# Turning the gated products of a feed-forward layer with VectorE and DMAs instead of TensorE

## The chip, the cores and the metric

One core of one Trainium2 chip runs the whole kernel. The metric is the device time of one execution in microseconds (us), taken as the median of the runs shown. TensorE multiplies matrices and writes to PSUM; VectorE (DVE in the profile) and ScalarE (ACT) move and combine tiles; SyncE (SP) issues the DMAs; GpSimd (POOL) has little to do here.

## The reference, cut to what matters

Two layers run over 256 tokens of width 2048. Each has a mixer (attention and a gated recurrence), a feed-forward part, and a gated embedding part. The change lies in the feed-forward part, whose inner width `D_FF` is 5632:

```python
h = rms_norm(x, pre_ffn_gain[i])
f = (jax.nn.silu(h @ w_ffn_gate[i]) * (h @ w_ffn_up[i])) @ w_ffn_down[i]
x = x + rms_norm(f, post_ffn_gain[i])
```

The product in the brackets (the gated product) comes out with tokens on the partitions. The multiplication by `w_ffn_down` sums over the 5632 columns, so it needs these columns on the partitions: the gated product has to be turned.

## The kernel before, in words

The 256 tokens are two tiles of 128, called t = 0 and t = 1. Every large product is made in strips of 512 output columns by `strip`. One strip walks down the rows of the weight matrix in steps of 256 rows; gate and up strips have 8 steps. For each step `load_w` loads 256x512 weights (512 KB) by one DMA on SP's queue into `wr` (4 buffers), and `split` makes of it two rounded float32r parts, `wh` by ScalarE and `wl` by VectorE (8 buffers each), which together keep the precision. TensorE then runs 12 matmuls per step, 6 for each t: left high by right high, left low by right high, left high by right low, for two blocks of 128 rows. The left operand is a turned, split tile `ck` (one high, one low).

The feed-forward part takes the 11 strips of the inner width in groups, `FF_GROUPS = (2, 3, 3, 3)`. For each strip of a group it runs a gate strip, whose end (`done_gate`, ScalarE) leaves silu of the gate in a `nat` tile, and an up strip, whose end (`done_up`) multiplies the two on VectorE. After the last strip of a group come four down strips (s = 0 to 3), which use the group's strips in order, two steps for each: a group of three has 6 steps in each down strip, and the third strip of the group is first used in step 5.

The gated product is turned by `split_T`: four TensorE transposes of 128x128 into a PSUM bank, then ScalarE copies the bank to the high part and VectorE subtracts to get the low part. `later(2, ...)` writes this code two steps after the end of the strip. Slots of a tag are given out and taken back by the framework: `nat` has 6, `ck` has 14.

The order on each engine is set when the program is built, by a list scheduler that follows the order of the code and its own estimates. On the chip, each engine works off its list in order and waits at semaphores; SP's list holds the weight loads, so a DMA that waits on SP holds back the loads behind it.

Of the kernel before, what the change touches and what calls it, by code (L numbers as in the profile page):

```python
# [8 lines left out]
F32 = mybir.dt.float32  # L9
# [6 lines left out]
P = 128  # L16
# [30 lines left out]
def decoder(ctx: ExitStack, tc: tile.TileContext, x, p, positions, w_in, attn_sinks,  # L47
# [3 lines left out]
    nc = tc.nc  # L51
# [5 lines left out]
    sp = ctx.enter_context(tc.tile_pool(name="sp", bufs=1))  # L57
    np_ = ctx.enter_context(tc.tile_pool(name="np", bufs=6))
    sm = ctx.enter_context(tc.tile_pool(name="sm", bufs=2))
    pacc = ctx.enter_context(tc.tile_pool(name="pacc", bufs=4, space=PSUM))  # L60
    pms = ctx.enter_context(tc.tile_pool(name="pms", bufs=4, space=PSUM))

    V, S, G, T = nc.vector, nc.scalar, nc.gpsimd, nc.tensor
# [7 lines left out]
    def later(n, fn):  # L71

        queue.append((clock[0] + n, fn))
# [28 lines left out]
    def nat(shape=(P, W), dt=F32):  # L102
        return np_.tile(list(shape), dt, tag="nat", name="nat")

    def bank(shape=(P, W)):
        return pms.tile(list(shape), F32, tag="ms", name="ms")
# [17 lines left out]
    ps = bank()  # L124
# [20 lines left out]
    def gain_cols(base, l, n):  # L145
        return gT[:, base + l * n: base + (l + 1) * n]
# [20 lines left out]
    def square_sum(src, acc, shape=(P, W)):  # L167
        j = np_.tile([P, W], F32, tag="junk", name="junk", bufs=1)
        S.activation(j[:, 0:shape[1]], src, AF.Square, accum_out=acc)  # L169

    def split(src, hi, lo):

        a = S.copy(hi, src)  # L173
        v = V.tensor_tensor(lo, src, hi.bitcast(F32), op=ALU.subtract)  # L174
        return a, v

    def split_wide(ps, gcols, h, lo):

        g = nat((P, 4, P))
        V.tensor_tensor(g, ps, gcols.unsqueeze(2).to_broadcast([P, 4, P]), op=ALU.mult)  # L180
        marks["x"], _ = split(g, h, lo)

    def split_T(src_blocks, gcols, hl, t, kt0=0, wide=False):

        n = len(src_blocks)
        ps = bank((P, n, P))
        for b, blk in enumerate(src_blocks):
            T.transpose(ps[:, b], blk, ident)  # L188
        h = hl[0][:, kt0:kt0 + n, t * P:(t + 1) * P]
        lo = hl[1][:, kt0:kt0 + n, t * P:(t + 1) * P]  # L190
        if gcols is None:
            split(ps, h, lo)
            return
        if wide:
            split_wide(ps, gcols, h, lo)
            return
        for b in range(n):
            g = gcols[:, b:b + 1]
            marks["x"] = S.activation(h[:, b], ps[:, b], AF.Copy, scale=g)  # L199
            V.scalar_tensor_tensor(lo[:, b], ps[:, b], g, h[:, b].bitcast(F32),  # L200
                                   op0=ALU.mult, op1=ALU.subtract)

    def new_ck():
        return [xp.tile([P, 4, SEQ], F32R, tag="ck", name="ck", bufs=14) for i in range(2)]

    def blocks4(a):
        return [a[:, b * P:(b + 1) * P] for b in range(4)]
# [11 lines left out]
    def strip(lhs, w, col, done, nch=8, row0=0, skew=0, psum=None, pre=None):  # L219

        ps = psum or [pacc.tile([P, W], F32, tag="acc", name=f"acc{t}") for t in range(NT)]
        ws = {}

        def part(t, c, lows=(0, 1)):
            hi, lo = ws[c]
            for k in range(2):
                kt = 2 * c + k
                xh, xl = (a[:, kt % 4, t * P:(t + 1) * P] for a in lhs[kt // 4])
                first, last = kt == 0, kt == 2 * nch - 1
                if 0 in lows:  # L230
                    T.matmul(ps[t], xh, hi[:, k], start=first, stop=False)  # L231
                    T.matmul(ps[t], xl, hi[:, k], start=False, stop=False)  # L232
                if 1 in lows:
                    marks[t, c] = T.matmul(ps[t], xh, lo[:, k], start=False, stop=last)  # L234

        for i in range(nch + skew):
            if pre:
                pre(i)
            if i < nch:
                with behind("x") if pre and i == 0 else nullcontext():  # L240
                    ws[i] = load_w(w, row0 // (2 * P) + i, col)
                if pre and i == 0:
                    for t in range(NT):
                        part(t, i, (0,))
                    for t in range(NT):
                        part(t, i, (1,))
                    tick()
                    continue
                part(0, i)
                if i == nch - 1:  # L250
                    done(0, ps[0])
            if i >= skew:
                part(1, i - skew)
            tick()
        done(1, ps[1])

    def load_gain(g, col):
        b = np_.tile([P, W], F32, tag="gB", name="gB", bufs=2)
        nc.sync.dma_start(b, g[col:col + W].partition_broadcast(P))
        return b  # L260

    def post_norm(mg, ss, t, nss, xT, gcols, wait):

        r = sum_rstd(ss[t], D, f"po{t}")
        for c in range(4):
            V.scalar_tensor_tensor(xr[t][c], mg[c][:, t], r[:, 0:1], xr[t][c],  # L266
                                   op0=ALU.mult, op1=ALU.add)

        def turn(cs):
            for c in cs:  # L270
                next_in(t, c, xT, gcols)
            for c in cs:
                square_sum(xr[t][c], nss[t][:, c:c + 1])
        later(wait, lambda: turn((0, 1)))
        later(wait + 1, lambda: turn((2, 3)))

    def next_in(t, c, xT, gcols, wide=False):
        split_T(blocks4(xr[t][c]), gcols[:, 4 * c:4 * c + 4], xT[c], t, wide=wide)
# [146 lines left out]
    for l in range(DEPTH):  # L425
# [385 lines left out]
        for s in range(4):  # L811
            gB = load_gain(post_mix_gain[l], s * W)

            def done(t, ps, s=s, gB=gB):
                if t == 0:
                    mg.append(sp.tile([P, NT, W], F32, tag="ABCD"[s], name=f"mg{s}"))
                V.tensor_tensor(mg[s][:, t], ps, gB, op=ALU.mult)
                square_sum(ps, ssm[t][:, s:s + 1])
                if s == 3:
                    post_norm(mg, ssm, t, ss, xT, gain_cols(32, l, 16), 4)  # L820
# [8 lines left out]
        for gi, glen in enumerate(FF_GROUPS):  # L829
            hid = []  # L830
            for j in range(glen):
                col = (ff0 + j) * W
                gate = {}

                def done_gate(t, ps):
                    gate[t] = nat()
                    S.activation(gate[t], ps, AF.Silu, scale=rx2(t)[:, 0:1])  # L837

                hl = new_ck()
                hid.append(hl)  # L840

                def done_up(t, ps):
                    V.scalar_tensor_tensor(gate[t], ps, rx2(t)[:, 0:1], gate[t],  # L843
                                           op0=ALU.mult, op1=ALU.mult)
                    later(2, lambda g=gate[t], hl=hl: split_T(blocks4(g), None, hl, t))

                strip(xT, w_ffn_gate[l], col, done_gate, skew=SKEW if ff0 + j == 0 else 0)
                strip(xT, w_ffn_up[l], col, done_up)
            last = gi == len(FF_GROUPS) - 1
            if last:  # L850
                nxT = [new_ck() for c in range(4)]
            for s in range(4):
                if gi == 0:
                    macc[s] = sp.tile([P, NT, W], F32, tag="ABCD"[s], name=f"macc{s}")
                if last:
                    gB = load_gain(post_ffn_gain[l], s * W)

                def done(t, ps, s=s):
                    m = macc[s][:, t]
                    if gi == 0:  # L860
                        S.copy(m, ps)
                        return
                    V.tensor_tensor(m, ps, m, op=ALU.add)  # L863
                    if last:
                        square_sum(m, ssf[t][:, s:s + 1])
                        V.tensor_tensor(m, m, gB, op=ALU.mult)
                        if s == 3:
                            post_norm(macc, ssf, t, nss, nxT, gain_cols(64, l, 16), (4, 3)[t])
                strip(hid, w_ffn_down[l], s * W, done, nch=2 * glen, row0=ff0 * W,
                      skew=4 if last and s == 3 else 0)  # L870
            ff0 += glen
# [67 lines left out]
```

## Time and profile before

| | us |
|---|---|
| median of 3 runs (2485.83 to 2488.48) | 2486.67 |
| the profiled execution, its own time | 2485.5 |
| span of its trace, first to last instruction | 2483.7 |
| TensorE busy in the span | 2464.8 (99%) |
| VectorE busy | 1445.0 (58%) |
| ScalarE busy | 1185.1 (48%) |

The profile's page lists busy time by engine, the chain of work that ended last, and groups of instructions. "L188" is line 188 of the kernel. A group's row shows its count, its busy time and the mean of one instruction in ns, then the idle time in front of it. Because matmuls overlap in the array, the distance from one start to the next is the price of a matmul, not its own duration. DMAs are shown by issue, with the median time from issue to landing.

### The profile page before, as it was taken

What the parts mean: (1) busy time and instruction counts of PE and PEld (TensorE: products, weight loads), DVE (VectorE), ACT (ScalarE), POOL (GpSimd) and SP (SyncE); (2) the same over time, 40 slices, a digit from 0 to 9 for tenths busy, and PEclk for the clock granted to TensorE, in tenths of its full rate; (3) what the DMA queues carried; (4) which work ended last, traced back from release to release, by engine and by line L of the source; (5) the groups of instructions that cost most, each with busy time, mean ns of one, the idle gap of its engine ahead of it and who ended that gap; (6) DMA issues with size and microseconds to landing.
All of it is one profiled execution on the core that took longest, in us unless ns stands there. A gap on an engine that the chain in (4) does not pass through costs nothing.

```text
span 2483.7 us, 30796 instructions
## 1 busy us (share of the span) xinstructions
PE 2464.8 (99%) x11597; PEld 2039.7 (82%) x11597; DVE 1445.0 (58%) x1901; ACT 1185.1 (48%) x1684; POOL 98.5 (4%) x213
## 2 busy tenths in 40 slices
PE   8999999999999999999999999999999999999999
PEld 6888887888888888887888888878888888888877
DVE  7786756544554454457567857565445545554574
ACT  6654446444434434446556444464444344444462
POOL 3100001000000000001010000010000000000010
PEclk9999999999999999999999999999999999999999
DMA  7445465666666666664564454656666666666653
GB/s 260 141 144 162 144 197 165 211 190 189 193 189 192 189 193 193 188 201 158 187 203 139 136 172 146 200 176 198 191 191 187 195 189 192 188 193 192 202 171 127
DMA packets 234262, 451.43 MB, mean 182 GB/s; under 512 B 14177, under 2 KB 15105, under 8 KB 234113
## 3 DMA queue, kind: packets, MB, share of 16 engines
q1 hardware_dynamic: 233808, 449.37, 59.1%
q8 instruction: 91, 1.49, 0.2%
q14 instruction: 59, 0.48, 0.1%
q10 hardware_dynamic: 240, 0.07, 0.0%
q0 software_dynamic: 64, 0.02, 0.0%
HBM read 447.31 MB, written 2.10 MB: 181 GB/s over the span
## 4 chain that ended last, share of the span: by engine, by line
PE 95%; DMA 2%; DVE 1%; ACT 1%; issue 0%; POOL 0%; SPq 0%; ACTq 0%; DVEq 0%; POOLq 0%
PE acc L231 29%; PE acc L232 29%; PE acc L234 29%; PE ms L188 2%; DMA wr<-in_w_in_dram 1%; PE ms L676 1%; PE ms L566 1%; DVE wl L174 1%; PE ms L515 0%; ACT wh L173 0%; PE ms L713 0%; ACT junk L169 0%; PE ms L741 0%; PE ms L232 0%; PE ms L234 0%
## 5 line engine op out<-in xcount | busy, mean ns | idle before, releaser
L174 DVE TENSOR_TENSOR wl<-wr,wh 128x1024 fp32r<-128x1024 f32 x840 | 1028.9, 1226 | 942.0 <-ACT wh L173 927.8
L173 ACT CAST wh<-wr 128x1024 fp32r<-128x1024 f32 x840 | 883.7, 1053 | 1121.2 <-PE acc L232 1068.6
L231 PE MATMUL acc<-wh,ck 128*128 128x512 f32 x3328 | 1309.8, 394 | 7.8 <-ACT ck L199 4.7
L232 PE MATMUL acc<-wh,ck 128*128 128x512 f32 x3328 | 1298.4, 390 | 0.9 <-DVE ck L200 0.8
L234 PE MATMUL acc<-wl,ck 128*128 128x512 f32 x3328 | 1297.3, 390 | 0.0
L231 PEld LDWEIGHTS acc<-wh,ck 128*128 128x128 f32 x3328 | 624.9, 188 | 139.5 <-ACT ck L199 10.1
L232 PEld LDWEIGHTS acc<-wh,ck 128*128 128x128 f32 x3328 | 625.6, 188 | 130.3 <-DVE ck L200 4.5
L234 PEld LDWEIGHTS acc<-wl,ck 128*128 128x128 f32 x3328 | 625.1, 188 | 130.8
L199 ACT ACTIVATE ck<-ms,gT 128x128 fp32r<-128x128 f32 x248 | 79.2, 368 | 35.2 <-DVE ck L200 27.7
L200 DVE SCALAR_TENSOR_TENSOR ck<-ms,gT,ck 128x128 fp32r<-128x128 f32 x248 | 75.8, 346 | 19.4 <-ACT ck L199 18.9
L159 POOL TENSOR_TENSOR tiny<-ssf 128x1 f32<-128x1 f32 x4 | 2.1, 535 | 1378.6 <-ACT junk L169 1378.3
L837 ACT ACTIVATE nat<-acc,ry 128x512 f32<-128x512 f32 x44 | 30.2, 687 | 10.7 <-PE acc L234 10.6
L863 DVE TENSOR_TENSOR macc<-acc,macc 128x512 f32<-128x512 f32 x48 | 33.0, 687 | 0.7
L169 ACT ACTIVATE junk<-x 128x512 f32<-128x512 f32 x48 | 30.2, 630 | 6.7 <-DVE x L266 4.1
L843 DVE SCALAR_TENSOR_TENSOR nat<-acc,ry,nat 128x512 f32<-128x512 f32 x44 | 32.4, 748 | 0.1
L174 DVE TENSOR_TENSOR ck<-ms,ck 128x512 fp32r<-128x512 f32 x44 | 30.1, 684 | 0.0
L188 PE MATMUL ms<-ident,x 128*128 128x128 f32 x192 | 27.8, 281 | 1.9 <-DVE x L896 1.2
L188 PEld LDWEIGHTS ms<-ident,x 128*128 128x128 f32 x192 | 22.6, 143 | 8.2 <-DVE x L896 2.4
L188 PEld LDWEIGHTS ms<-ident,nat 128*128 128x128 f32 x184 | 22.8, 139 | 6.4 <-DVE ck L200 0.4
L188 PE MATMUL ms<-ident,nat 128*128 128x128 f32 x184 | 28.0, 272 | 0.0
L459 POOL TENSOR_TENSOR nat<-nat 128x256 f32<-128x256 f32 (+1 forms) x24 | 22.7, 968 | 109.0 <-DVE nat L452 97.6
L534 ACT ACTIVATE nat<-nat,tiny 128x128 f32<-128x128 f32 x64 | 24.8, 390 | 3.9 <-DVE tiny L531 3.6
(198 smaller groups left out, 884.1 us busy)
## 6 DMA issues: line engine op xcount, KB each, us to landing
wr<-in_w_in_dram SPq DMA_DIRECT2D x176, 512.0 KB, 3.8
wr<-in_w_ffn_gate_dram SPq DMA_DIRECT2D x176, 512.0 KB, 3.8
wr<-in_w_ffn_up_dram SPq DMA_DIRECT2D x176, 512.0 KB, 3.7
wr<-in_w_ffn_down_dram SPq DMA_DIRECT2D x176, 512.0 KB, 3.7
wr<-in_w_out_dram SPq DMA_DIRECT2D x64, 512.0 KB, 4.1
wr<-in_w_ple_gate_dram SPq DMA_DIRECT2D x64, 512.0 KB, 4.3
wr<-in_w_ple_proj_dram SPq DMA_DIRECT2D x8, 512.0 KB, 4.2
x<-in_x_dram SPq DMA_DIRECT2D x8, 256.0 KB, 7.6
```

The costliest lines, as they stand in the source:

```text
L169: S.activation(j[:, 0:shape[1]], src, AF.Square, accum_out=acc)
L173: a = S.copy(hi, src)
L174: v = V.tensor_tensor(lo, src, hi.bitcast(F32), op=ALU.subtract)
L188: T.transpose(ps[:, b], blk, ident)
L199: marks["x"] = S.activation(h[:, b], ps[:, b], AF.Copy, scale=g)
L200: V.scalar_tensor_tensor(lo[:, b], ps[:, b], g, h[:, b].bitcast(F32), op0=ALU.mult, op1=ALU.subtract)
L231: T.matmul(ps[t], xh, hi[:, k], start=first, stop=False)
L232: T.matmul(ps[t], xl, hi[:, k], start=False, stop=False)
L234: marks[t, c] = T.matmul(ps[t], xh, lo[:, k], start=False, stop=last)
L837: S.activation(gate[t], ps, AF.Silu, scale=rx2(t)[:, 0:1])
L843: V.scalar_tensor_tensor(gate[t], ps, rx2(t)[:, 0:1], gate[t], op0=ALU.mult, op1=ALU.mult)
L863: V.tensor_tensor(m, ps, m, op=ALU.add)
```

## The change

The gated product is turned in two stages. VectorE turns each 32x32 block in place (`V.transpose`). The 4x4 arrangement of the blocks is then turned by DMAs: one stores the 256 KB tile to a scratch tile `turn` in DRAM, and four load it back, 64 KB each, into 32 partitions each, in runs of 128 floats (512 bytes). All five are issued on SP's queue; the four loads wait for the store to land. ScalarE and VectorE then split the loaded tile as before, now from SBUF. It is done for every strip of every group but the second strip of the group of two: 10 strips of 11, 2 tiles each, 2 layers, which is 40 turns; 4 stay on TensorE. The splitting code is written three steps after the end of a strip, not two.

```diff
+    dp = ctx.enter_context(tc.tile_pool(name="dp", bufs=4, space=bass.MemoryType.DRAM))
...
+    def shuffled(src):
+        b = nat()
+        V.transpose(b.rearrange("p (q k j) -> p k q j", q=4, k=4),
+                    src.rearrange("p (k q j) -> p k q j", k=4, q=4))
+        m = dp.tile([4, 32, 4, P], F32, tag="turn", name="turn")
+        nc.sync.dma_start(m.rearrange("a i q f -> (a i) (q f)"), b)
+        d = nat()
+        for q in range(4):
+            nc.sync.dma_start(d[q * 32:(q + 1) * 32].rearrange("i (a f) -> i a f", a=4),
+                              m[:, :, q].rearrange("a i f -> i a f"))
+        return d
+
+    def split_shuffled(d, hl, t):
+        cols = slice(t * P, (t + 1) * P)
+        split(d.rearrange("p (a k j) -> p k a j", a=4, k=4),
+              *(a[:, :, cols].rearrange("p k (a j) -> p k a j", a=4) for a in hl))
...
-                def done_up(t, ps):
+                def done_up(t, ps, hl=hl, gate=gate, j=j):
                     V.scalar_tensor_tensor(gate[t], ps, rx2(t)[:, 0:1], gate[t],
                                            op0=ALU.mult, op1=ALU.mult)
-                    later(2, lambda g=gate[t], hl=hl: split_T(blocks4(g), None, hl, t))
+                    if glen == 2 and j == 1:
+                        later(2, lambda g=gate[t], hl=hl: split_T(blocks4(g), None, hl, t))
+                        return
+                    d = shuffled(gate[t])
+                    later(3, lambda: split_shuffled(d, hl, t))
```

The scheduler places the new instructions. The place that matters most is the end of the last up strip of a group of three, where the down strips follow at once.

SP's queue, before: the loads of the last gate and up strip of the first group of three, of the down strips, and of the group behind them.

```order
L212 DMA wr<-in_w_ffn_gate_dram 128x2x512 x8
L212 DMA wr<-in_w_ffn_up_dram 128x2x512 x8
L212 DMA wr<-in_w_ffn_down_dram 128x2x512 x24
L212 DMA wr<-in_w_ffn_gate_dram 128x2x512 x8
L212 DMA wr<-in_w_ffn_up_dram 128x2x512 x8
```

SP's queue in the changed kernel, among the 24 loads of the down strips that follow that group's last up strip (line numbers are 20 or more higher from here on):

```order
L232 DMA wr<-in_w_ffn_down_dram 128x2x512 x11
L211 DMA turn<-nat 128x512
L232 DMA wr<-in_w_ffn_down_dram 128x2x512
L214 DMA nat<-turn 32x4x128 x4
L211 DMA turn<-nat 128x512
L232 DMA wr<-in_w_ffn_down_dram 128x2x512 x2
L214 DMA nat<-turn 32x4x128 x4
L232 DMA wr<-in_w_ffn_down_dram 128x2x512 x10
```

The two stores and eight loads of the two turns stand between the 11th and the 15th weight load of the down strips; the same pattern, 11 weight loads past the end of the strip, stands at the other turns.

VectorE, before, behind the end of the same up strip (the first row is the product for t = 1; `ck<-ms` makes the low part of a turned tile from PSUM):

```order
L843 SCALAR_TENSOR_TENSOR nat_5525<-acc1_5528,ry1_3960,nat_5525 128x512
L174 TENSOR_TENSOR wl_5824<-wr_5821,wh_5823 128x1024
L174 TENSOR_TENSOR wl_5842<-wr_5839,wh_5841 128x1024
L174 TENSOR_TENSOR ck_5362<-ms_5695,ck_5361 128x4x128
L174 TENSOR_TENSOR wl_5860<-wr_5857,wh_5859 128x1024
L174 TENSOR_TENSOR ck_5362<-ms_5720,ck_5361 128x4x128
```

VectorE in the changed kernel, at the same place (`ck<-nat` makes the low part from the loaded tile; `macc<-acc` is the end of the first down strip for t = 0):

```order
L863 SCALAR_TENSOR_TENSOR nat<-acc_5554,ry_3962,nat 128x512
L208 STREAM_TRANSPOSE nat<-nat 128x4x4x32
L175 TENSOR_TENSOR wl<-wr,wh 128x1024 x2
L208 STREAM_TRANSPOSE nat<-nat 128x4x4x32
L175 TENSOR_TENSOR wl<-wr,wh 128x1024 x2
L175 TENSOR_TENSOR ck<-nat,ck 128x4x128
L175 TENSOR_TENSOR wl<-wr,wh 128x1024
L887 TENSOR_TENSOR macc_4435<-acc_5719,macc_4435 128x512
L175 TENSOR_TENSOR wl<-wr,wh 128x1024
L175 TENSOR_TENSOR ck<-nat,ck 128x4x128
```

The two block transposes came in, and the two low parts moved from behind the second and third weight split to behind the fourth and sixth.

TensorE, before, in the first down strip of that group: the first transposes stand behind step 1 (and the second behind step 2), and in step 6 each t follows the other.

```order
L234 MATMUL acc1_5676<-wl_5680,ck_4747 128x512
L188 MATMUL ms_5695<-ident_90,nat_5517 128x128 x4
L231 MATMUL acc0_5675<-wh_5704,ck_4747 128x512
L232 MATMUL acc0_5675<-wh_5704,ck_4748 128x512
L234 MATMUL acc0_5675<-wl_5705,ck_4747 128x512
```

TensorE in the changed kernel, in step 2 of the second down strip (acc1_5836 is that strip's t = 1, acc1_5720 the first strip's; ck_5397 and ck_5398 are the high and low part of the turned third strip):

```order
L251 MATMUL acc1_5836<-wh_5857,ck_4757 128x512
L251 MATMUL acc1_5720<-wh_5799,ck_5397 128x512
L252 MATMUL acc1_5836<-wh_5857,ck_4758 128x512
L254 MATMUL acc1_5836<-wl_5858,ck_4757 128x512
L251 MATMUL acc1_5836<-wh_5857,ck_4757 128x512
L252 MATMUL acc1_5836<-wh_5857,ck_4758 128x512
L254 MATMUL acc1_5836<-wl_5858,ck_4757 128x512
L252 MATMUL acc1_5720<-wh_5799,ck_5398 128x512
```

The transposes are gone, and the 12 matmuls of t = 1 on the third strip moved from steps 5 and 6 of the first down strip to behind step 1 of the second; those of t = 0 still stand in steps 5 and 6.

## The prediction

> **What bounds the kernel now.** I read the page's engine totals and its chain of waits first, then one window of the feed-forward part, then who waited there, and last the timelines of single engines at one turn. From the page, its first part and the chain by engine:
>
> ```profile
> PE 2464.8 (99%) x11597; PEld 2039.7 (82%) x11597; DVE 1445.0 (58%) x1901; ACT 1185.1 (48%) x1684; POOL 98.5 (4%) x213
> ...
> PE 95%; DMA 2%; DVE 1%; ACT 1%; issue 0%; POOL 0%; SPq 0%; ACTq 0%; DVEq 0%; POOLq 0%
> ```
>
> TensorE is the chain. The window 600 to 760 us, and the waits from 500 to 1000 us on the engines and on SP's queue (engine, tile and line, releaser: us in total, times, longest):
>
> ```profile
> 600.00:760.00 160.00, 160.00 (x715) 132.46 (x714) 81.41 (x74) 65.76 (x67) 0.00 (x0) 1.00 0.62 191
> ...
> ACT wh L173 <- PE acc L232: 283.1, 181, 2.7
> DVE wl L174 <- ACT wh L173: 246.1, 173, 2.4
> PEld acc L232 <- DVE ck L174: 0.2, 1, 0.2
> ...
> SPq L212 <- DVE wl L174: 420.8, 182, 3.7
> ```
>
> In the feed-forward part TensorE is busy 160.00 of 160.00 us at a granted clock of 1.00, VectorE 81.41, ScalarE 65.76, the DMA engines 0.62. Everybody waits for TensorE: ScalarE's split for a weight buffer that TensorE frees, VectorE's split for ScalarE's, SP's loads for VectorE's. So time taken off TensorE there comes off the end, as long as its operands stay in time.
>
> **What is removed.** TensorE's timeline at the turn behind the first group of three (start, duration):
>
> ```profile
> 677.35 0.39 PE L231 MATMUL acc<-wh,ck 128*128 128x512 f32 x1
> ...
> 679.85 0.39 PE L234 MATMUL acc<-wl,ck 128*128 128x512 f32 x1
> 680.08 0.60 PE L188 MATMUL ms<-ident,nat 128*128 128x128 f32 x4
> 680.43 0.47 PE L231 MATMUL acc<-wh,ck 128*128 128x512 f32 x1
> 680.75 0.39 PE L232 MATMUL acc<-wh,ck 128*128 128x512 f32 x1
> ```
>
> and ScalarE's weight splits, each started by TensorE's end of a step:
>
> ```profile
> 677.33 1.06 ACT L173 CAST wh<-wr 128x1024 fp32r<-128x1024 f32 x1 [1.67 <-PE acc L232]
> 680.05 1.05 ACT L173 CAST wh<-wr 128x1024 fp32r<-128x1024 f32 x1 [1.66 <-PE acc L232]
> ...
> 683.23 1.05 ACT L173 CAST wh<-wr 128x1024 fp32r<-128x1024 f32 x1 [1.65 <-PE acc L232]
> ...
> 686.45 1.05 ACT L173 CAST wh<-wr 128x1024 fp32r<-128x1024 f32 x1 [1.68 <-PE acc L232]
> 689.17 1.05 ACT L173 CAST wh<-wr 128x1024 fp32r<-128x1024 f32 x1 [1.67 <-PE acc L232]
> ```
>
> A step without transposes takes 680.05 − 677.33 = 2.72 us (689.17 − 686.45 too). The two with four transposes take 3.18 and 3.22, so four transposes cost 0.46 to 0.50, mean 0.48. From the single rows they cost at least 680.43 − 680.08 = 0.35; the rest sits in the slower start of the next matmul. 40 turns x 0.48 = 19.2 us off TensorE; the low end is 40 x 0.35 = 14.0, the high end 40 x 0.50 = 20.0. Nothing else of TensorE's work changes. ScalarE's and VectorE's copies out of PSUM become copies out of SBUF.
>
> The Trainium skill, page "VectorE: DVE Perf Modes", section "The three transpose paths", gives TensorE 390 ns for a 128x128 bf16 transpose and advises TensorE for that size. By that figure 160 transposes would be 62 us, an estimate. The trace has 0.12 us each where they follow one another, and that decides.
>
> **What is added, off TensorE.** The means of one instruction, the DMAs' sizes with median landing, and SP's price of one issue (min/median/max, ns):
>
> ```profile
> L174 DVE TENSOR_TENSOR wl<-wr,wh 128x1024 fp32r<-128x1024 f32 x840 | 1028.9, 1226 | 942.0 <-ACT wh L173 927.8 <-PE ms L624 5.9 <-DMA lrows<-in_hgrn_lb_logits_dram 1.2
> L174 DVE TENSOR_TENSOR ck<-ms,ck 128x512 fp32r<-128x512 f32 x44 | 30.1, 684 | 0.0
> L174 DVE TENSOR_TENSOR ck<-nat,ck 128x512 fp32r<-128x512 f32 x2 | 1.4, 724 | 0.1
> L173 ACT CAST ck<-nat 128x512 fp32r<-128x512 f32 x2 | 1.2, 618 | 3.8 <-DVE nat L180 3.8
> ...
> wr<-in_w_ffn_down_dram SPq DMA_DIRECT2D x176, 512.0 KB, 3.7
> out_dram<-x SPq DMA_DIRECT2D x7, 256.0 KB, 2.0
> nat<-in_p_dram SPq DMA_DIRECT2D x4, 128.0 KB, 3.7
> L212 SPq DMA_DIRECT2D wr<-in_w_ffn_down_dram x176: 367/368/379, 472.7 to 2342.8; - x176
> ```
>
> The trace has no block transpose. Its nearest rows are VectorE's 128x512 passes at 0.68 and, as the upper bound, the 128x1024 pass at 1.23; I take 0.69. 40 x 0.69 = 28 us on an engine that is idle for 49% of the window: hidden, not on the chain. ScalarE's copy from SBUF takes 0.62, VectorE's low part 0.72: no more than 0.1 us each over before, hidden likewise. SP issues 5 more DMAs per turn, 5 x 0.37 = 1.85 us of a queue that waited 420.8 us of 500. Bytes: 40 x 512 KB, or 20 MB, what the window's rate of 191 GB/s moves in 0.1 ms, spread over two feed-forward parts.
>
> **The waits that are added.** A store waits on SP for VectorE's transpose, the four loads wait for the store to land, and both hold back the weight loads behind them. The changed order puts the store 11 weight loads past the strip's end, where SP waits anyway. VectorE's and SP's timeline at this place:
>
> ```profile
> 675.69 1.23 DVE L174 TENSOR_TENSOR wl<-wr,wh 128x1024 fp32r<-128x1024 f32 x1 [1.50 <-ACT wh L173]
> 676.84 1.47 DVE L843 SCALAR_TENSOR_TENSOR nat<-acc,ry,nat 128x512 f32<-128x512 f32 x2
> ...
> 676.95 0.37 SPq L212 DMA_DIRECT2D wr<-in_w_ffn_down_dram  x1
> ```
>
> The load at 676.95 is the 11th of the down strips (its buffer came free with the VectorE row above). Call TensorE's end of the up strip T = 677.35. Products done: 676.84 + 1.47, T+0.96. Block transpose of t = 0: T+1.65. Store issued there, loads after it. Behind these stand weight loads that TensorE needs 12 steps, over 30 us, later; each is late by a few us at most. So weights cost nothing; their cover is the 8 split buffers and 4 raw ones, and it is gone only if SP is held for some 20 us.
>
> The turned tile itself is the risk. Where a group's third strip ends, the down strips follow at once and use it in step 5: T + 4 x 2.72 = T+10.9 for t = 0, the low part one matmul (0.23) later, T+11.1. That is 6 places (3 groups, 2 layers); at the other 28 turns the use is at least a gate and an up strip, 16 steps or 43 us, later. For t = 1 the changed order asks for it only past step 1 and half of step 2 of the second down strip, about 6.6 steps or T+17.9.
>
> VectorE's own order sets a floor: the low part of t = 0 stands behind the fourth weight split, which starts at ScalarE's copy for the step that ends at T + 3 x 2.72 = T+8.2, so ends at about 8.2 + 1.05 + 1.2 = T+10.4; plus 0.72 gives T+11.1, just in time. The DMA path must beat that. How long a store takes beside weight loads, from the output stores near the end (three windows around them, min/median/max us to landing) and SP's issues ahead of them:
>
> ```profile
> 2398.53 0.37 SPq L212 DMA_DIRECT2D wr<-in_w_ple_gate_dram  x1
> 2401.64 0.36 SPq L898 DMA_DIRECT2D out_dram<-x  x1
> ...
> 2428.93 0.37 SPq L212 DMA_DIRECT2D wr<-in_w_ple_gate_dram  x1
> 2430.34 0.36 SPq L898 DMA_DIRECT2D out_dram<-x  x1
> ...
> DMA to landing us min/median/max: 2.0/2.0/2.0
> ...
> DMA to landing us min/median/max: 4.3/4.5/4.8
> ```
>
> The store issued 3.1 us after a weight load landed in 2.0 us; the two of the window from 2430, the first of them 1.4 us after one, in 4.3 to 4.8. Ours comes 677.35 + 1.65 − 676.95 = 2.05 us after one: between, and I take 3.4. The four loads have no row of their own kind; the nearest is `nat<-in_p_dram`, 3.7 us, the bound below is the store's 2.0, the one above the slowest weight load of the window 500 to 1000 us:
>
> ```profile
> DMA to landing us min/median/max: 3.5/3.7/5.4
> ```
>
> I take 3.7, as the row nearest in size. Last load issued 3 x 0.37 = 1.1 us after the store landed: T + 1.65 + 3.4 + 1.1 + 3.7 = T+9.85, high part at 10.5, low part by 11.2: TensorE waits 0.1. At the late ends (4.8 and 5.4) it is T+12.95, low part at 14.3, a wait of 3.2; at the early ones 0. For t = 1 the low part stands behind another weight split whose buffer TensorE frees after 6 steps, T+16.3, and comes at about T+19.3, when it is wanted: 0 to 0.2. I take 0.3 for both together: 6 x 0.3 = 2 us, ends 0 and 6 x 3.4 = 20.
>
> The page "DMA: Bandwidth & Descriptors" of the Trainium skill, section "Anatomy of one DMA", fits 2.0 us plus bytes over 436 GB/s: an estimate of 2.6 us for the store and 2.2 for a load, by which there would be no wait at all and 19 us gained. The stores here took up to 4.8 beside weight loads, so the rows bound the wait, not the fit.
>
> **Sum.** 2485.5 − 19.2 + 2 = 2468.3 for an execution like the profiled one, which lies 1.2 below the median shown; so 2469.5 as a median, forecast 2470. A change under 0.2% (5 us) can't be told from none.
>
> **Rivals.** (1) The turned tile is late by more than the sum allows at the 6 places. For it: store and loads follow each other and each can take 5 us beside weight traffic. Against: the late ends of both at once are needed. A wait of 1 to 2 us each gives 2485.5 − 19.2 + 6 to 12, so 2473 to 2480 as a median. (2) No change: waits of 2.5 to 4 us each, or only 14.0 us taken off and 1.5 to 3 waited each: 2482 to 2491. For it: the slowest rows of the trace added up give 3.2; against: they fell on single transfers. (3) Slower: loads in 512-byte runs into 32 partitions are a kind of their own and land more slowly than any row. It decides from 9.85 + 4 = about T+14 on, where 6 waits pass 24 us; landing 10 us late gives 2486.7 − 19 + 6 x 10 = 2527. Against: the DMA engines are 62% busy and 64 KB is an eighth of a weight load.
>
> The Trainium skill's page "VectorE: DVE Perf Modes" warns, in the section named above, that a plain DMA which transposes by its access pattern runs 19 times slower than the crossbar's transpose if the innermost stride is large. This would bring rival 3 about; here the innermost run is 128 contiguous floats, and no run shown has such a DMA.
>
> **Chances.** Forecast, waits under 1 us (2466 to 2473): 0.62. Rival 1: 0.19. Rival 2: 0.11. Rival 3: 0.08. Faster is the first two, 0.81; same 0.11; slower 0.08. The range leaves out rival 3 and most of rival 2 above, and below what 20.0 us off without a wait would give (2486.7 − 20.0 = 2466.7, with 1 us for the spread of runs): 2465.5 to 2483.
>
> **What would show it.** Right: no `nat` transposes on TensorE in the feed-forward part but 16 and those of `p`, steps of 2.72 us throughout, TensorE's waits for `ck` near zero; block transposes near 0.69 us; 40 stores landing in 2 to 5 us. Wrong: TensorE waiting in step 5 of a group's first down strip for `ck` by ScalarE or VectorE, these in turn for the `turn` loads; or waits for `wh` and `wl` two strips later, if SP was held longer than I read.

## The result and the profile after

The changed kernel takes 2468.52 us (median of 4 runs, 2468.28 to 2469.23), beside 2486.97 for the kernel before in the same runs (2485.83 to 2488.48): a ratio of 0.9926, interval 0.9909 to 0.9943. The forecast was 2470, range 2465.5 to 2483. The profiled execution took 2468.36 us, its span 2466.6, 17.1 less than before; the sum of the prediction had 17.2.

The page's engine totals and chain by engine, as shown before the change:

```profile
PE 2447.2 (99%) x11437; PEld 2023.1 (82%) x11437; DVE 1465.8 (59%) x1941; ACT 1186.8 (48%) x1684; POOL 101.2 (4%) x213
...
PE 95%; DMA 2%; DVE 1%; ACT 1%; issue 0%; POOL 0%; SPq 0%; ACTq 0%; DVEq 0%; POOLq 0%
```

TensorE has 160 matmuls fewer (11597 to 11437) and 17.6 us less busy time; VectorE has 40 instructions and 20.8 us more. TensorE is still the chain.

The new work, by groups of instructions and by DMA issues (count, KB each, median us to landing):

```profile
L208 DVE STREAM_TRANSPOSE nat<-nat 128x512 f32<-128x512 f32 x40 | 28.1, 703 | 0.0
L175 DVE TENSOR_TENSOR ck<-nat,ck 128x512 fp32r<-128x512 f32 x42 | 28.8, 686 | 0.0
...
wr<-in_w_ffn_down_dram SPq DMA_DIRECT2D x176, 512.0 KB, 4.3
...
turn<-nat SPq DMA_DIRECT2D x40, 256.0 KB, 2.7
nat<-turn SPq DMA_DIRECT2D x160, 64.0 KB, 3.3
```

The same window of the feed-forward part as before, and SP's queue from 500 to 1000 us:

```profile
600.00:760.00 160.00, 160.00 (x706) 132.11 (x705) 85.21 (x80) 66.77 (x68) 0.00 (x0) 1.00 0.69 208
...
SPq L232 <- DVE wl L175: 357.6, 168, 5.1
SPq L214 <- DMA turn<-nat: 16.3, 14, 2.0
SPq L211 <- DVE nat L208: 11.3, 7, 1.6
```

TensorE is busy throughout, as before. SP waits 63 us less for weight buffers (420.8 to 357.6): that slack took in the new DMAs. The DMA engines' share rose from 0.62 to 0.69, and the median landing of a down load from 3.7 to 4.3 us, with no wait of TensorE for weights in this stretch.

The length of one layer's feed-forward part is read from VectorE: the first product of gate and up, and the last addition into the result of the down strips, t = 1. First the kernel before, then the changed one:

```profile
455.30 1.54 DVE L843 SCALAR_TENSOR_TENSOR nat<-acc,ry,nat 128x512 f32<-128x512 f32 x2
...
1143.25 0.68 DVE L863 TENSOR_TENSOR macc<-acc,macc 128x512 f32<-128x512 f32 x1
```

```profile
455.80 1.54 DVE L863 SCALAR_TENSOR_TENSOR nat<-acc,ry,nat 128x512 f32<-128x512 f32 x2
...
1134.99 0.69 DVE L887 TENSOR_TENSOR macc<-acc,macc 128x512 f32<-128x512 f32 x1
```

So 687.95 us became 679.19, 8.8 less, in a layer with 20 of its 22 turns changed; layer 2 gives 8.7. The two layers account for the whole gain.

Now the risk, the turn behind the first group of three. SP's, ScalarE's and VectorE's timelines there; the up strip ends at T = 674.95, where ScalarE's first row starts:

```profile
676.57 0.34 SPq L211 DMA_DIRECT2D turn<-nat  x1
677.68 0.37 SPq L232 DMA_DIRECT2D wr<-in_w_ffn_down_dram  x1
679.68 1.75 SPq L214 DMA_DIRECT2D nat<-turn  x4
681.53 0.38 SPq L211 DMA_DIRECT2D turn<-nat  x1
682.00 1.10 SPq L232 DMA_DIRECT2D wr<-in_w_ffn_down_dram  x2
683.71 1.75 SPq L214 DMA_DIRECT2D nat<-turn  x4
```

```profile
674.95 1.06 ACT L174 CAST wh<-wr 128x1024 fp32r<-128x1024 f32 x1 [1.67 <-PE acc L252]
...
684.06 0.62 ACT L174 CAST ck<-nat 128x512 fp32r<-128x512 f32 x1
```

```profile
684.19 1.23 DVE L175 TENSOR_TENSOR wl<-wr,wh 128x1024 fp32r<-128x1024 f32 x1 [1.49 <-ACT wh L174]
685.34 0.68 DVE L175 TENSOR_TENSOR ck<-nat,ck 128x512 fp32r<-128x512 f32 x1
```

The store of t = 0 goes out at T+1.6 and the loads at T+4.7, released by its landing: 3.1 us. ScalarE's copy of the loaded tile starts at T+9.1 with no idle time in front of it, so the loads had landed. VectorE's low part stands behind the fourth weight split and ends at 685.34 + 0.68 = T+11.1. TensorE's row of that use:

```profile
686.08 0.49 PE L252 MATMUL acc<-wh,ck 128*128 128x512 f32 x1
686.41 0.40 PE L254 MATMUL acc<-wl,ck 128*128 128x512 f32 x1
```

The usual distance of two starts is 0.227; here it is 0.33, a wait of 0.10 us. The use of t = 1 shows another 0.11. That is all the waiting at this place.

### The profile page after: what moved, and what is told of

Same layout as the page of the kernel before. It is cut to its first block, busy times and chain, and to the rows that moved or that the text cites. A ratio compares the mean times of both kernels' runs of the same rounds, so it can differ in the third digit from the quotient of the medians.

```text
span 2466.6 us, 30888 instructions
## 1 busy us (share of the span) xinstructions
PE 2447.2 (99%) x11437; PEld 2023.1 (82%) x11437; DVE 1465.8 (59%) x1941; ACT 1186.8 (48%) x1684; POOL 101.2 (4%) x213
## 4 chain that ended last, share of the span: by engine, by line
PE 95%; DMA 2%; DVE 1%; ACT 1%; issue 0%; POOL 0%; SPq 0%; ACTq 0%; DVEq 0%; POOLq 0%
PE acc L251 30%; PE acc L252 30%; PE acc L254 29%; DMA wr<-in_w_in_dram 1%; PE ms L696 1%; PE ms L586 1%; PE ms L189 1%; DVE wl L175 1%; PE ms L535 0%; ACT wh L174 0%; PE ms L733 0%; ACT junk L170 0%; PE ms L761 0%; PE ms L254 0%; PE ms L251 0%
## 5 line engine op out<-in xcount | busy, mean ns | idle before, releaser
L189 PEld LDWEIGHTS ms<-ident,x 128*128 128x128 f32 x192 | 22.6, 143 | 8.1 <-DVE x L920 2.4
L175 DVE TENSOR_TENSOR ck<-nat,ck 128x512 fp32r<-128x512 f32 x42 | 28.8, 686 | 0.0
L208 DVE STREAM_TRANSPOSE nat<-nat 128x512 f32<-128x512 f32 x40 | 28.1, 703 | 0.0
L174 ACT CAST ck<-nat 128x512 fp32r<-128x512 f32 x42 | 26.0, 619 | 4.0 <-DVE nat L181 3.6
```

## The experiments

Four theories are told apart: the gain is TensorE's time for the transposes; it is something else (the order, for instance); the added DMA path costs time on the chain; and, if the path is late, what it costs and what hides it. For each kernel the time is a median beside runs of the kernel before on the same chip (medians of 2485.45 to 2486.6 us).

### e5_te_twice and e4_no_turning: the price of a turn

e5, on the kernel before, repeats the four transposes of all 44 turns:

```diff
+        for b, blk in enumerate(src_blocks if again else ()):
+            T.transpose(ps[:, b], blk, ident)
```

> In the kernel before, TensorE does the four transposes of each of the 44 turns of the gated products twice. Theory: a turn costs 0.35 us where the transposes follow one another and 0.48 with the slower start of the matmul behind them, so 44 x 0.35 to 0.48 = 15.4 to 21.1 us more: 2502 to 2508. Rival (the 0.48 us are mostly the change from matmuls to transposes and back, which is paid once): under 2495.

e4, on the kernel before, leaves the turning out and splits the product as it lies:

```diff
-                    later(2, lambda g=gate[t], hl=hl: split_T(blocks4(g), None, hl, t))
+                    later(2, lambda g=gate[t], hl=hl: split(
+                        g.rearrange("p (k j) -> p k j", k=4), hl[0][:, :, cols], hl[1][:, :, cols]))
```

> The turning is left out: the gated product is split as it lies, so the feed-forward result is another; no transposes, no DMAs for it. Theory: 44 x 0.48 = 21.1 us under before, 2465.9, and 1.9 (the 4 turns left) plus 0.6 to 1.3 (waits at six places) under the changed kernel. Rival (the DMAs cost more than waits at six places, for example through the weight loads that land later): 2462 or less.

Measured: e5 2504.43, ratio 1.0074 (1.006 to 1.0087), 18.6 us over before, or 0.42 per doubled turn. e4 2464.0, ratio 0.9908 (0.9894 to 0.9921), 22.6 under, or 0.51 per turn, and 1.9 less than expected. Its feed-forward part, read from the same two rows:

```profile
455.50 1.54 DVE L843 SCALAR_TENSOR_TENSOR nat<-acc,ry,nat 128x512 f32<-128x512 f32 x2
...
1132.80 0.68 DVE L865 TENSOR_TENSOR macc<-acc,macc 128x512 f32<-128x512 f32 x1
```

677.30 us, 10.65 under before for 22 turns: 0.484 each. The prediction read 0.48 from single steps. (The two layers make 21.3 us, which is also the difference of the two traces' spans, 2483.7 and 2462.4; the medians add 1.3.)

### e3_added_alone: the added work without the gain

The changed kernel, in which the block transposes and all five DMAs run but their result is unused, and TensorE turns too:

```diff
-                    d = shuffled(gate[t])
-                    later(3, lambda: split_shuffled(d, hl, t))
+                    shuffled(gate[t])
+                    later(2, lambda g=gate[t], hl=hl: split_T(blocks4(g), None, hl, t))
```

> The block transposes, the 40 stores and the 160 loads are added to the kernel before; their result is not used and TensorE turns as before. Theory: all of it lies beside TensorE's work, so the time is that of before, 2487, within 1 us. Rival (the added work has a price of its own that the changed kernel pays too, on VectorE 28 us, on SP's queue 74 us, or on the weight loads): clearly over 2490.

Measured: 2487.52, ratio 1.0003 (0.9995 to 1.0012). The traffic, SP's issues and VectorE's 28 us cost nothing that can be measured; the feed-forward part of its trace takes 687.96 us, before 687.95. What can still cost is a tile that is wanted before it is there.

### e1_third_on_te and e2_all_turned: fewer and more turns

e1 leaves the last strip of every group on TensorE, and so turns no tile at the 6 risky places; e2 takes the exception out and turns all 44.

```diff
-                    if glen == 2 and j == 1:
+                    if j == glen - 1:
```

> The last strip of every group stays on TensorE: 28 turns go by DMA, none of them at the six places where the turned tile is asked for soon. Theory (a turn taken off TensorE is worth 0.48 us, its added work is hidden, and only the six places can wait): 28 x 0.48 = 13.4 us under the 2487.0 of before, 2473.5, and no wait of TensorE for a turned tile. Rival (the waits at the six places eat what the 12 turns there bring): 2468 to 2469, as the changed kernel, or less.

> All 44 turns go by DMA, also the second strip of the group of two, which its down strips ask for two steps on instead of four. Theory: 4 x 0.48 = 1.9 us less on TensorE than the changed kernel; the scheduler puts the second down strip's first two steps in front, so that the tile is asked for at about T+10 instead of T+5.4, against T+11 when it is ready: 1 us of wait at each of 2 places, a little more for t = 1. 2467 to 2471. Rival (the wait is set by the distance in the code, T+5.4): 2 x 5.6 us more, 2477 to 2478.

Measured: e1 2471.95 (ratio 0.9938, 0.9926 to 0.9951), 14.65 under before, 0.52 for each of 28 turns, a little better than the theory's 2473.5. The 12 turns at the risky places thus bring 3.4 us, 0.29 each and not 0.48, which leaves some 2.3 us for waits there. The traces say the same: e1's feed-forward part takes 681.24 us, what e4's 677.30 and 8 turns of 0.484 on TensorE make (681.17), so nothing waits in it.

e2 2465.81 (0.9914, 0.9901 to 0.9928), better than expected, 2.7 under the changed kernel, where four turns of 0.48 make 1.9. In the traces its two feed-forward parts are 0.6 and 0.9 us shorter (678.60 and 678.37, against 679.19 and 679.28), 0.38 for each of the four turns, at two further places where the down strips follow at once. The rest lies outside these parts and is not explained.

### e6_two_trips: the path made twice as long

```diff
-        return d
+        m2 = dp.tile([P, W], F32, tag="again", name="again")
+        nc.sync.dma_start(m2, d)
+        e = nat()
+        for q in range(4):
+            nc.sync.dma_start(e[q * 32:(q + 1) * 32], m2[q * 32:(q + 1) * 32])
+        return e
```

> Each of the 40 turned tiles makes a second trip through DRAM (one more store, four more loads), so it lands some 6 to 9 us later for t = 0 and, since the trips follow one another on SP's queue, 10 to 15 us later for t = 1. Theory: 34 of the 40 turns hide it; at the six places the scheduler has put more of the next two down strips in front, so TensorE waits little for the tile itself, but up to four of the eight split weight buffers stay held; 0 to 3 us at each of six places, 2468 to 2487. Rival (each us of lateness costs a us at the six places, 6 to 15 us each): 2505 to 2560. Second rival (a turn may be as late as it likes): 2468.5.

Measured: 2468.29 (0.9928, 0.9915 to 0.994), as the changed kernel. The second store and its loads take these times to landing:

```profile
again<-nat SPq DMA_DIRECT2D x40, 256.0 KB, 5.1
nat<-again SPq DMA_DIRECT2D x160, 64.0 KB, 4.4
```

ScalarE's copies of the two turned tiles at the place looked at above, where the up strip now ends at T = 673.88:

```profile
693.88 0.62 ACT L174 CAST ck<-nat 128x512 fp32r<-128x512 f32 x1
...
710.36 0.62 ACT L174 CAST ck<-nat 128x512 fp32r<-128x512 f32 x1
```

They begin at T+20.0 and T+36.5, in the changed kernel at T+9.1 and T+17.4. That the tiles come 11 and 19 us later cost nothing, because the scheduler, which counts a DMA with its estimate, placed the work anew (VectorE's first addition of a down strip moved from T+13.9 to T+24.9): TensorE now does the first four steps of the second down strip ahead of steps 5 and 6 of the first for t = 0, and asks for t = 1 only in the strip after. So the distance at the 6 places is not set by the code. It is set by the order that the scheduler makes. The time is the second rival's, but a turn may be late only because the order moves with it, as the next run shows.

### e8_order_kept: the same path, the order not moved

The second down strip of a group of three is held behind the end of the first, so that TensorE asks for t = 1 after step 6 of t = 0, at T+13.6 instead of T+17.9:

```diff
+                with (tc.issue_after(marks[1, 2 * glen - 1].ins) if s == 1 and glen == 3
+                      else nullcontext()):
-                strip(hid, w_ffn_down[l], s * W, done, nch=2 * glen, row0=ff0 * W,
```

> In the groups of three, TensorE's matmuls of the second down strip may not be put in front of the end of the first, so that both tiles of the turned third strip are asked for in steps 5 and 6 as the code has them: t = 0 at T+10.9, t = 1 at T+13.6. In the changed kernel's trace the loads of t = 1 land at about T+15.7. Theory (the scheduler's order hides the path of t = 1): a wait of 15.7 + 0.6 + 0.7 - 13.6 = 3.4 us at most, less what a nearer place in ScalarE's and VectorE's order brings, 2 to 3.4 us at six places: 2480 to 2489, most of the gain gone. Rival (the order is of no matter, t = 1 has slack): 2468 to 2470.

Measured: 2493.01 (1.0028, 1.0017 to 1.004), beyond the expected range: 24.5 us over the changed kernel, 4.1 at each place. The profiled execution is the slowest of six (2490.8 to 2496.3), 27.9 over the changed kernel's. TensorE's waits in the whole run (us, times, longest), and four windows from its first stall on (the columns are TensorE, weight load, VectorE, ScalarE and GpSimd busy, then the granted clock as a share of TensorE's full speed, DMA share and GB/s):

```profile
PE acc L251 <- ACT ck L174: 16.2, 6, 3.2
```

```profile
688.00:690.00 2.00, 0.15 (x1) 0.00 (x0) 0.69 (x1) 0.00 (x0) 0.00 (x0) 1.00 1.03 273
690.00:692.00 2.00, 0.84 (x2) 0.40 (x2) 0.69 (x1) 0.62 (x1) 0.00 (x0) 0.60 0.53 200
692.00:697.00 5.00, 5.00 (x12) 3.93 (x13) 1.25 (x2) 1.49 (x2) 0.00 (x0) 0.50 0.00 0
697.00:700.00 3.00, 3.00 (x14) 2.39 (x14) 1.86 (x2) 0.89 (x2) 0.00 (x0) 0.96 0.65 181
```

The waits explain 16.2 us of the 27.9. Most of the rest is of the kind of the third row: after the stall TensorE runs at a granted clock of 0.50, and 5 us of work there do what 2.5 did before. Four of the other five stalls are followed by such a stretch too (0.57 over the 4 us from 1093, 1929 and 2332 us, 0.66 over the 5 us from 2130), and all five cost 10.3 us, which leaves 1.4. The expectation had priced a stall at its own length.

### e7_loads_on_pool and e9_pool_late_use: the path made later than the order allows for

e7 issues the four loads on GpSimd's queue instead of SP's, so as to take them out of the way of the weight loads:

```diff
-            nc.sync.dma_start(d[q * 32:(q + 1) * 32].rearrange("i (a f) -> i a f", a=4),
+            nc.gpsimd.dma_start(d[q * 32:(q + 1) * 32].rearrange("i (a f) -> i a f", a=4),
```

> The four loads of each turn are issued by GpSimd instead of SP, so that no weight load waits behind a store's landing. Theory (SP's queue is never held long enough to matter): the same time as the changed kernel, 2468.5 within 1 us. Rival (the weight loads behind the turn cost something): 1 us or more under it.

Measured: 2490.0 (1.0015, 1.0007 to 1.0024), a miss by 21.5 us. The landings; TensorE's and ScalarE's waits in the whole run; GpSimd's and ScalarE's timelines at the first place, where the up strip ends at 674.62; and windows of TensorE's clock:

```profile
turn<-nat SPq DMA_DIRECT2D x40, 256.0 KB, 4.1
nat<-turn POOLq DMA_DIRECT2D x160, 64.0 KB, 4.3
```

```profile
PE acc L251 <- ACT ck L174: 14.6, 7, 2.7
...
ACT ck L174 <- DMA nat<-turn: 98.1, 40, 4.4
```

```profile
679.89 2.17 POOL L214 DMA_DIRECT2D nat<-turn  x4 [33.79 <-DVE wl L175]
```

```profile
674.62 1.05 ACT L174 CAST wh<-wr 128x1024 fp32r<-128x1024 f32 x1 [1.67 <-PE acc L252]
...
686.81 0.62 ACT L174 CAST ck<-nat 128x512 fp32r<-128x512 f32 x1 [2.98 <-DMA nat<-turn]
```

```profile
684.00:689.00 5.00, 2.98 (x12) 1.93 (x11) 2.37 (x3) 1.57 (x2) 2.17 (x4) 1.00 0.90 290
689.00:693.00 4.00, 4.00 (x12) 3.14 (x11) 1.22 (x2) 0.62 (x1) 0.00 (x0) 0.57 0.48 157
...
885.00:889.00 4.00, 1.75 (x7) 0.92 (x6) 1.13 (x3) 1.57 (x2) 1.16 (x3) 1.00 0.80 254
889.00:893.00 4.00, 3.40 (x15) 2.44 (x14) 1.60 (x2) 0.00 (x0) 1.02 (x2) 1.00 0.60 174
...
1088.00:1092.00 4.00, 3.29 (x7) 2.37 (x8) 1.92 (x2) 1.56 (x2) 1.96 (x4) 0.58 0.48 154
1925.00:1929.00 4.00, 4.00 (x12) 3.13 (x11) 1.02 (x2) 0.62 (x1) 0.00 (x0) 0.59 0.52 153
2324.00:2328.00 4.00, 4.00 (x11) 3.13 (x12) 1.23 (x1) 0.74 (x2) 0.33 (x1) 0.57 0.68 197
```

The store landed 1.4 us later than in the changed kernel, a load 1.0 later, and the four issues took longer on GpSimd (2.17 us beside 1.75 on SP). At the first place ScalarE's copy of t = 0 began at T+12.2, not T+9.1. The scheduler kept TensorE's use of it in step 5, about T+11. TensorE waited 14.6 us in 7 stalls, and four of these were followed by some 3.4 us at half clock (0.57 over 4 us), which cost 0.43, 0.42, 0.41 and 0.43 of 4 us, 6.8 in all: 21.4 together, of the 23.8 us by which the profiled execution (2492.17, among runs from 2485.7 to 2495.3) lies over the changed kernel's. But another account was open: ScalarE waited 98.1 us in order for the loads, with weight splits behind it. e9 tells them apart. It keeps the loads on GpSimd and writes the first two down strips of a group of three so that steps 1 to 4 of both come before steps 5 and 6 of either; in the last group it scales the first strip's result with the gains of the second, with the same work.

```diff
+                if glen == 3 and s < 2:
+                    pair.append(part_strip(hid, w_ffn_down[l], s * W, done, ff0 * W))
+                    if s == 1:
+                        for cs in ((0, 1, 2, 3), (4, 5)):
+                            for run in pair:
+                                run(cs)
+                    continue
```

> As e7_loads_on_pool (the four loads are issued by GpSimd), but the first two down strips of a group of three are written so that TensorE does steps 1 to 4 of both before steps 5 and 6 of either. The turned tile of the third strip is then first used at T + 8 x 2.72 = T+21.8 instead of T+10.9; in e7 ScalarE's copy of it ended at T+13.3 (t = 0). Theory (what costs in e7 is that TensorE asks for the tile before it has landed, and the half clock behind such a stall): no stall at the 6 places, no half clock, 2466 to 2469. Rival (the loads by GpSimd cost in themselves: ScalarE waits 98 us in order for them and holds back the weight splits, or the weight loads land later): most of the 21.5 us stay, 2483 to 2490.

Measured: 2465.55 (0.9916, 0.9902 to 0.9931). The stores and loads land as late as in e7, ScalarE waits as long, and the time is 24 us shorter:

```profile
turn<-nat SPq DMA_DIRECT2D x40, 256.0 KB, 4.3
nat<-turn POOLq DMA_DIRECT2D x160, 64.0 KB, 4.5
```

```profile
ACT ck L174 <- DMA nat<-turn: 99.7, 39, 4.9
```

Its feed-forward part takes 678.4 us, 0.1 over e4's 677.30 and the two turns of 0.484 that stay on TensorE. So neither GpSimd's issue nor ScalarE's waiting costs anything by itself. What cost 21.5 us in e7 was that TensorE asked for the tile before it had landed, with the half clock that followed.

### e10_attention_too, e11_more_turned, e12_order_written: how far it goes

e10 is e2 with the same turning for 16 tiles of the mixer (the outputs of attention and recurrence), e11 adds 16 more (the recurrence's gate z and the attention's q), and e12 is e10 with the order written as in e9, with the loads on SP's queue.

```diff
+                d = shuffled(o)
+                later(4, lambda: scale_shuffled(
+                    d, gain_cols(112, l, 8)[:, 4 * s.grp:4 * s.grp + 4], mix[c], t))
-                later(2, lambda: split_T(blocks4(o), gain_cols(112, l, 8)[:, 4 * s.grp:4 * s.grp + 4],
-                                         mix[c], t))
```

> As e2_all_turned (2465.8), and in the mixer the attention's and the recurrence's gated outputs, 16 tiles of 128x512 in all, are turned by VectorE and DMAs too; the split with its gains reads the loaded tile. Theory (each turn hidden gives 0.42 to 0.52 us): 16 x 0.47 = 7.5, so 2457 to 2460. Rival (in the mixer the tile is wanted sooner and the scheduler has less other work for TensorE; 4 places a layer where TensorE would stall 2 us and run at half clock for 3.4): 2470 to 2490.

> As e10_attention_too, and 16 tiles more: the recurrence's gate z (8) and the attention's q (8). Theory: another 7.5 us off, 2449 to 2453. Rival: these stand in chains of the mixer (gate, then products with it; q, then the scores), with little other work ready, so each DMA path of 6 to 9 us shows in part: above e10, 2460 to 2500.

> As e10_attention_too (2460.5), loads on SP's queue, and the first two down strips of a group of three written as in e9_pool_late_use: steps 1 to 4 of both, then steps 5 and 6 of both. From first up-strip end to the end of the feed-forward part e10 took 678.3 us in each layer and the kernel with nothing turned 677.3. Theory (what is left there is waits for the turned tile at the 3 places, and the written order removes them): 2 x 1.0 us off, 2458 to 2459.5. Rival (what is left is not waiting, but slower weights or the like): 2460 to 2461, no difference that can be told from e10.

Measured: e10 2460.52 (0.9896, 0.9881 to 0.9911), 5.3 under e2, 0.33 per turn, just outside what was expected. The traces show 3.05 us less up to the first feed-forward part and 3.59 less between the two, 0.38 and 0.45 per turn, and 1.2 more behind the second, where nothing was changed (e3 has 1.1 more there than before). e11 2458.61 (0.989, 0.9873 to 0.9906): 1.9 for 16 turns where 7.5 were expected, and its runs (2456.29 to 2461.04) overlap with e10's (2459.6 to 2461.1). One window over most of layer 2's mixer, e10 first, then e11:

```profile
1140.00:1680.00 540.00, 537.64 (x2685) 447.46 (x2684) 368.06 (x598) 291.11 (x499) 34.79 (x60) 1.00 0.57 181
```

```profile
1140.00:1680.00 540.00, 535.23 (x2654) 444.04 (x2653) 373.61 (x605) 292.29 (x498) 34.85 (x59) 1.00 0.60 189
```

TensorE has 31 matmuls less and is idle 2.4 us more, and between the two feed-forward parts e11 gains only 0.1 us: there a part of the DMA path shows, as the rival said. In that layer ScalarE's copies of the turned q wait 4.4 us for the loads, and TensorE waits 0.9 for such a copy. e12 took 2458.57 (0.989, 0.9874 to 0.9907), within its theory's range: its feed-forward part takes 677.4 us where e10's took 678.3, against 677.3 with nothing turned. So TensorE's waits for the turned tile were the last 0.9 us of a layer.

## Why the prediction was right, point by point

- **What is removed.** 0.48 us per turn, read from the steps of ScalarE's timeline; e4 gives 0.484 in the feed-forward part. For the transposes alone, back to back, the single rows say 0.35 and e5 0.42; the steps also hold the slower start of the next matmul. (The 0.12 us that the prediction gives for one transpose where they follow one another is a quarter of 0.48, with that slower start in it; e5 makes it 0.11.) 40 x 0.48 = 19.2 stands.
- **What is added, hidden.** VectorE's block transpose took 0.70 (0.69 estimated), the store 2.7 as a median (3.1 at the place worked out, 3.4 taken), a load 3.3 (3.7 taken). e3 shows that all of it is hidden, SP's part with it.
- **The floor at T+11.1.** Reached to the tenth, and VectorE's order, not the DMA path, set it: ScalarE's copy began at T+9.1 where the sum had the loads landing at T+9.85. The wait was 0.10, as forecast, but the forecast had it from the DMA path (low part by T+11.2): that the figures agree is luck.
- **The sum of the waits.** 2 us were taken. e4's layer plus two turns that stay on TensorE is 677.30 + 0.97 = 678.27; the changed kernel's is 679.19: 0.92 per layer, 1.8 in all, or 0.31 at each of the six places. At the place looked at, the waits make 0.21 of the 0.3 taken.
- **Rival 1 and the reason.** The forecast held, but the account of t = 1 was thinner than it reads. It took the use at T+17.9 from the changed order as given. e6 and e8 show that this order is the cover: it follows the estimated landing, and without it the gain is gone. On SP's queue a late tile was therefore less likely than the rivals' chances had it, as far as the scheduler's estimates hold; this is inferred from these runs, not shown. In e7 the order did not allow for the later landing.
- **The price of rival 3.** This was mis-sized, though it did not come to bear: the prediction turns lateness into time one to one (10 us late, 6 x 10). In e7 and e8 a stall of 1.8 to 3.2 us was followed in 9 of 12 cases by a stretch at half clock that cost 1.7 us more (once 3.4), so the point from which the change loses lies nearer than T+14. At the first place e7's copy began at T+12.2, and in the whole run the gain was lost.

The Trainium skill, page "DMA: Bandwidth & Descriptors", section "Anatomy of one DMA", states its fit for DMAs that GpSimd issues; the prediction used it for SP's queue, as estimates of 2.6 us for the store and 2.2 for a load. With weight loads going at the same time the medians on SP were 2.7 and 3.3, and the loads that GpSimd itself issued in e7 and e9 took 4.3 and 4.5: it comes near for the store and is short for the loads on either queue. The Trainium skill's page "TensorE: Matmul & The Clock Gate", section "HAM oscillation — how this bites in real kernels", warns of TensorE gaps over about 3.4 us. Here idle gaps of 1.8 to 3.2 us brought the half clock in 9 of 13 cases (the window at 885 us holds one that did not), so the measurement puts the limit lower for this kernel. Nor need it be one gap: in e1, e2 and e3 the clock was halved from about 27 us on with no single gap above 1 us, behind 3.6 us in which TensorE was busy for 2.1 to 2.2.

## What to carry to other kernels

Where TensorE is the chain, a turn that VectorE and DMAs can do is worth just what its steps on TensorE take (0.48 us for four blocks of 128x128 in this feed-forward part), provided the turned tile lands before TensorE's list asks for it. Look up that moment in the order made, not in the code; where the landing is uncertain, write other steps of TensorE's work in front of the use, as e9 and e12 do. Price a stall of TensorE of about 2 us and more at its length plus 1.7 us of half clock, which followed in most cases here. In the mixer a turn brought less than in the feed-forward part: 0.33 us in e10, about 0.1 for the further turns of e11.

## What the runs showed of the hardware that was not expected

- After an idle gap of 1.8 to 3.2 us TensorE's granted clock fell to 0.50 for about 3.4 us in 9 of 13 cases of e7, e8 and e11, not counting the first 30 us of a run (in one of the nine, shown from 688 us, for about 6.8); gaps of up to 1.5 us never did it in these three runs past that point.
- The four loads issued by GpSimd landed in 4.3 us (3.3 on SP), and the stores on SP in 4.1 (2.7), with a time of 2.17 us for the four issues beside 1.75. Why the stores grew too was not tried.
